# Output and down products that finish one token tile first, and a feed-forward that starts tile by tile, in a two-block transformer kernel

## Chip, cores and metric

The kernel runs on one core of a Trainium2 chip. The metric is the device time of one execution in microseconds. The engines are TensorE (PE; its weight loads are shown as PEld), VectorE (DVE), ScalarE (ACT), GpSimd (POOL) and SyncE (SP), which issues the weight transfers. Each engine runs its instructions in a fixed order.

## What is computed

256 latent tokens and 256 context tokens of width 1024 go through a first block of two layers; a second block of two other layers follows. Only the first block's products are touched by the change. Of the reference:

```python
def _post(x, f, gate, g, b):
    return _layernorm(ALPHA * x + gate * f, g, b)
def _modulate(x, shift, scale):
    return _layernorm(x) * (1.0 + scale) + shift
def _merge(o_att, o_gla, r, glu, gates, p):
    ...
    return (g_att * y_att + g_gla * y_gla + g_conv * y_conv) @ p['w_out']
def _ffn(h, p):
    return (jax.nn.silu(h @ p['w_ff_gate']) * (h @ p['w_ff_up'])) @ p['w_ff_down']
...
        if last:
            mem = _context_memory(hc, p)
        else:
            yc, mem = _context_mixer(hc, p)
            xc = _post(xc, yc, mod_c[2], ln1_g[l], ln1_b[l])
            xc = _post(xc, _ffn(_modulate(xc, mod_c[3], mod_c[4]), p), mod_c[5], ln2_g[l], ln2_b[l])
        x = _post(x, _latent_mixer(_modulate(x, sh1, sc1), mem, cos, sin, p), g1, ln1_g[l], ln1_b[l])
        x = _post(x, _ffn(_modulate(x, sh2, sc2), p), g2, ln2_g[l], ln2_b[l])
```

## The kernel before

Tokens lie on the partitions in two token tiles of 128, t0 and t1. All products are in fp32 accuracy: each operand is split into a high and a low part, and `mm3` (L216) makes three matmuls of them, hi by hi (L220), hi by lo (L221) and lo by hi (L222). A weight is loaded by SP as 512 KB (`raw`), cast to `hi` by ScalarE (L210, 128x1024) and subtracted to `lo` by VectorE (L213, two of 128x512); `weights` does that. There are four buffers for `raw`, three for `hi` and two for `lo`; with a pool and a tag given, the parts go to other memory instead.

The mixer's output product has 1024 columns in two halves c=0 and c=1, and eight blocks of 128 along the contraction, of which `weights` brings four at a time: a block (c, h) is thus half of the contraction of half of the columns. `out(c)` (L1549) is called by `post` (L1003) for c=0 and then c=1. It takes two PSUM banks, one for each token tile; in `gemm_t` each weight block is used for t0 and then t1, but the last `tail` blocks are done for t0 and then for t1. For c=1 the last two blocks are such a tail.

`post` works on each half as it is ready (`part`): L1012 multiplies by the gate, L1013 adds the residual and sums, GpSimd forms the mean (L1016), ScalarE squares (L1017), and after c=1 VectorE and GpSimd (L1023 to L1027) form the variance. `end` normalises with the wide VectorE operations L1042 and L1044. Then `ln` (L960, ScalarE's square L961, GpSimd's L274, L275, L963) and the write L969 (ScalarE, t0) or L967 (VectorE, t1) give the feed-forward's input; `to_hT` transposes it on TensorE (L984, two tiles into one PSUM bank), modulates (L989 on ScalarE, L987 on VectorE) and splits it (L310 ScalarE, L311 VectorE) into the operand `b`.

`ffn` (L1557) makes 11 features of 512 numbers, each of two weights e=0 (gate) and e=1 (up), in `g` and `t` banks, 48 matmuls of 256 columns a weight; then the down product with 22 blocks along the contraction, six weights a column half, again through `post`. In layer 0 latent and context tokens share one `ffn` (T=512), and `begin` (L1575) makes three weights' products of the context ahead. In layer 1 the context is not needed (T=256, `cn` is None), and after it the second block starts (its norm: L369, L376; transposes L385; splits L313, L314).

The pools of the mixer and of the feed-forward are opened one after the other on the same memory, so that a tile of the second waits until what lay there is read. What stands where in an engine's queue is decided when the kernel is built, by a scheduler that lays the program out over the engines and gives each engine a fixed order.

## Time and profile before

| what | value |
|---|---|
| runs of before | 2748.75, 2737.08, 2747.66 us; median 2747.66 |
| the profiled execution | 2742.06 us, span 2740.2 us |
| TensorE busy | 2640.3 us, 96% of the span |
| VectorE busy | 1955.6 us, 71% |
| ScalarE busy | 1383.8 us, 50% |
| GpSimd busy | 136.0 us, 5% |
| mean granted TensorE clock | 0.98 |

TensorE's share says little by itself, since it is near the span everywhere but at the seams between stages. Those are read in windows of some tens of microseconds, with the time in which TensorE worked and the clock that was granted to it (1.0 is 2.4 GHz, 0.5 is 1.2 GHz), and then in the timeline of an engine, where a value in brackets is the idle time ahead of an instruction and what ended it.

### The profile page before, as it was taken

What the parts mean: (1) busy time and instruction counts of PE and PEld (TensorE: products, weight loads), DVE (VectorE), ACT (ScalarE), POOL (GpSimd) and SP (SyncE); (2) the same over time, 40 slices, a digit from 0 to 9 for tenths busy, and PEclk for the clock granted to TensorE, in tenths of its full rate; (3) what the DMA queues carried; (4) which work ended last, traced back from release to release, by engine and by line L of the source; (5) the groups of instructions that cost most, each with busy time, mean ns of one, the idle gap of its engine ahead of it and who ended that gap; (6) DMA issues with size and microseconds to landing.
All of it is one profiled execution on the core that took longest, in us unless ns stands there. A gap on an engine that the chain in (4) does not pass through costs nothing.

```text
span 2740.2 us, 44882 instructions
## 1 busy us (share of the span) xinstructions
PE 2640.3 (96%) x17024; PEld 2260.7 (83%) x17024; DVE 1955.6 (71%) x3942; ACT 1383.8 (50%) x2524; POOL 136.0 (5%) x280
## 2 busy tenths in 40 slices
PE   7999999999999999999999999989999999999999
PEld 5877999977889888887797898879976699776897
DVE  4988977888866633345688997666666698556895
ACT  3555565545545422234745654544454566544663
POOL 0010011000001100002100100010010000000000
PEclk9999999999999999999999999989999999998999
DMA  7566556565535522222555433545554256542454
GB/s 255 185 229 205 170 171 217 173 205 177 178 116 193 185 85 93 93 96 91 155 170 202 156 128 116 169 154 193 186 186 156 89 185 195 173 149 80 167 192 155
DMA packets 127912, 443.29 MB, mean 162 GB/s; under 512 B 14888, under 2 KB 19112, under 8 KB 127696
## 3 DMA queue, kind: packets, MB, share of 16 engines
q1 hardware_dynamic: 127696, 440.43, 48.7%
q8 instruction: 134, 2.20, 0.3%
q14 instruction: 82, 0.67, 0.1%
HBM read 435.09 MB, written 5.28 MB: 161 GB/s over the span
## 4 chain that ended last, share of the span: by engine, by line
PE 87%; DVE 4%; DMA 3%; ACT 3%; issue 1%; POOL 1%; SPq 0%; DVEq 0%; POOLq 0%; ACTq 0%
PE g L221 20%; PE g L220 20%; PE g L222 20%; PE t L221 3%; PE t L222 3%; PE t L220 3%; DMA raw<-in_w_dram 2%; PE g L919 2%; PE t L1142 2%; PE t L1168 1%; PE t L1270 1%; PE t L1255 1%; PE t L1105 1%; DVE lo L213 1%; PE g L663 1%
## 5 line engine op out<-in xcount | busy, mean ns | idle before, releaser
L213 DVE TENSOR_TENSOR lo<-raw,hi 128x512 fp32r<-128x512 f32 (+2 forms) x1280 | 825.3, 684 | 350.4 <-issue 156.7
L210 ACT CAST hi<-raw 128x1024 fp32r<-128x1024 f32 (+2 forms) x644 | 671.9, 1045 | 723.9 <-PE g L221 252.3
L220 PE MATMUL g<-b,hi 128*128 128x256 f32 (+1 forms) x2912 | 831.1, 287 | 2.5 <-ACT hi L210 1.8
L221 PE MATMUL g<-b,hi 128*128 128x256 f32 (+1 forms) x2912 | 827.7, 286 | 2.7 <-DVE b L311 2.6
L222 PE MATMUL g<-b,lo 128*128 128x256 f32 (+1 forms) x2912 | 822.3, 287 | 1.6 <-DVE lo L213 1.6
L220 PEld LDWEIGHTS g<-b,hi 128*128 128x128 f32 x2912 | 548.2, 189 | 13.5 <-ACT b L310 2.4
L221 PEld LDWEIGHTS g<-b,hi 128*128 128x128 f32 x2912 | 548.6, 188 | 12.4 <-DVE b L311 4.3
L222 PEld LDWEIGHTS g<-b,lo 128*128 128x128 f32 x2912 | 541.5, 188 | 11.0 <-DVE lo L213 2.7
L1282 DVE SCALAR_TENSOR_TENSOR yc<-yc,vec,yc 128x256 f32<-128x256 f32 x720 | 345.7, 480 | 10.9
L221 PE MATMUL g<-lo,b 128*128 128x512 f32 (+2 forms) x712 | 271.8, 382 | 1.8 <-DVE lo L213 1.7
L220 PE MATMUL g<-hi,b 128*128 128x512 f32 (+2 forms) x712 | 253.5, 376 | 11.8 <-ACT hi L210 6.2
L222 PE MATMUL g<-hi,b 128*128 128x512 f32 (+2 forms) x712 | 264.2, 371 | 0.5 <-DVE b L314 0.4
L220 PEld LDWEIGHTS g<-hi,b 128*128 128x128 f32 x712 | 134.0, 191 | 38.6 <-ACT hi L210 7.0
L221 PEld LDWEIGHTS g<-lo,b 128*128 128x128 f32 x712 | 135.7, 191 | 30.5 <-DVE lo L213 6.3
L222 PEld LDWEIGHTS g<-hi,b 128*128 128x128 f32 x712 | 135.3, 190 | 22.2 <-DVE b L314 1.1
L220 PE MATMUL t<-b,hi 128*128 128x256 f32 (+1 forms) x336 | 111.9, 333 | 0.0
L221 PE MATMUL t<-b,hi 128*128 128x256 f32 (+1 forms) x336 | 111.9, 333 | 0.0
L222 PE MATMUL t<-b,lo 128*128 128x256 f32 (+1 forms) x336 | 111.7, 332 | 0.0
L919 PE MATMUL g<-raw,cs 128*32 128x512 f32 x384 | 84.4, 637 | 12.4 <-DMA raw<-in_w_dram 12.2
L477 DVE SCALAR_TENSOR_TENSOR s<-g,vec,s 128x255 f32<-128x255 f32 (+1 forms) x176 | 84.2, 478 | 6.0 <-ACT s L475 3.8
L221 PEld LDWEIGHTS t<-b,hi 128*128 128x128 f32 x336 | 63.2, 188 | 7.5
L220 PEld LDWEIGHTS t<-b,hi 128*128 128x128 f32 x336 | 63.1, 188 | 7.4
(421 smaller groups left out, 3924.1 us busy)
## 6 DMA issues: line engine op xcount, KB each, us to landing
raw<-in_w_dram SPq DMA_DIRECT2D x772, 512.0 KB
b<-in_row_dram SPq DMA_DIRECT2D x16, 512.0 KB
b<-in_ctx_dram SPq DMA_DIRECT2D x4, 512.0 KB
ends<-st SPq DMA_DIRECT2D x8, 256.0 KB
st<-ends SPq DMA_DIRECT2D x8, 256.0 KB
b<-in_x_dram SPq DMA_DIRECT2D x4, 512.0 KB
b<-ctx SPq DMA_DIRECT2D x4, 512.0 KB
raw<-in_w_dram SPq DMA_DIRECT2D x4, 426.0 KB
```

Of the source, the lines that this page charges most:

```text
L210: self.nc.scalar.copy(hi[:, :m], p)
L213: self.nc.vector.tensor_sub(lo[:, q], p[:, q], hi[:, q].bitcast(F32))
L220: t.matmul(ps, a[0], b[0], start=first, stop=False)
L221: t.matmul(ps, a[0], b[1], start=False, stop=False)
L222: t.matmul(ps, a[1], b[0], start=False, stop=last)
L477: nc.vector.scalar_tensor_tensor(c[:, m, j:], ps[:, m, :256 - j], cw[:, ft, 2 - j:3 - j], c[:, m, j:], op0=ALU.mult, op1=ALU.add)
L663: nc.tensor.matmul(ps[:, b], qk['nq', a * per + b][s, t * 128:t * 128 + 128], qk[kn, 0][s, :nk], start=False, stop=b == per - 1)
L919: nc.tensor.matmul(ps[32 * q:32 * q + 32], self.cs[:, h * 4 + q], raw[:, q % 2 * 512:q % 2 * 512 + 512], start=h == 0, stop=h == 1, tile_p ...
L1105: nc.tensor.matmul(p[:, h], kw[:, d, h * 128:h * 128 + 128], vg[:, h * 256:h * 256 + 256], start=True, stop=True)
L1142: nc.tensor.matmul(o, w, self.U[d][:, b * 256:b * 256 + n], start=d + i == 0, stop=d + i == 2)
L1168: nc.tensor.matmul(ps[:, a, h], G[h][b][:, a] if b < 3 else kT[:, h, ts], G[h][b][:, 2 + a], start=True, stop=True)
L1282: e.scalar_tensor_tensor(o, y[:, j:j + 256], w[:, j:j + 1], o, op0=ALU.mult, op1=ALU.add)
```

## The change

In all three full mixers `out` takes all four PSUM banks at once. The block (0, 0) is done for both token tiles; then the three other blocks (0, 1), (1, 0), (1, 1) are done for t0 and after that for t1. Their weights lie at the same time in three places: the second in pool P under 'p', the third under 'mk' and 'st', the last in the usual `hi` and `lo`. t0's products end 36 matmuls of 512 columns ahead of t1's; before, 24 in the code.

In layer 1's `ffn` a new `tile_hT` transposes and modulates one token tile at a time, and the first feature is made token tile by token tile: 96 matmuls of 256 columns as before, now with the tokens on the partitions, then four transposes back and a copy. The weights of its second half go to tiles 'z'.

In layer 1's down product the tail for c=1 is three blocks long instead of two, the last two in 'z' and 'w'; t0 ends 30 matmuls ahead instead of 18. Line numbers grow by one behind L206, by 19 behind `tile_hT`: L1012 becomes L1031, L1013 L1032, L1023 to L1025 L1042 to L1044, L1042 L1061, L1044 L1063, L1073 to L1075 L1092 to L1094.

```diff
--- before.py
+++ after.py
@@ -205,8 +205,9 @@
             for at in range(0, n, cols):
                 m = min(cols, n - at)
                 p = raw[:, at:at + m]
-                hi = self.tile(pool or self.slot(), [128, cols], F32R, tag or 'hi')
-                lo = self.tile(pool or self.W, [128, cols], F32R, tag or 'lo')
+                th, tl = tag if isinstance(tag, tuple) else (tag or 'hi', tag or 'lo')
+                hi = self.tile(pool or self.slot(), [128, cols], F32R, th)
+                lo = self.tile(pool or self.W, [128, cols], F32R, tl)
                 self.nc.scalar.copy(hi[:, :m], p)
                 for h in range(0, m, 512):
                     q = slice(h, min(m, h + 512))
@@ -261,8 +262,8 @@
         hs = list(range((n + 3) // 4))
         if n % 4:
             hs[-2:] = hs[:-3:-1]
-        own = hs[len(hs) - last:]
-        return [(4 * h, lambda h=h: self.weights(src(h), min(4, n - 4 * h), ncol, *(at if h in own else ()))) for h in hs]
+        own = dict(zip(hs[len(hs) - last:], at if at and isinstance(at[0], tuple) else (at,) * last))
+        return [(4 * h, lambda h=h: self.weights(src(h), min(4, n - 4 * h), ncol, *own.get(h, ()))) for h in hs]
 
 
     def small(self, fam, n=8):
@@ -990,6 +991,24 @@
             a = slice(kp * 2, kp * 2 + 2)
             self.split_to(hi[:, a, c0:c0 + 256], lo[:, a, c0:c0 + 256], h)
 
+    def tile_hT(self, xn, t, s, sh, sc, hi, lo):
+
+        nc = self.nc
+        ts = slice(t * 128, t * 128 + 128)
+        for c in range(2):
+            ps = self.tile(self.PT, [128, 4, 128], F32, 't')
+            h = self.tile(self.A, [128, 4, 128], F32, 'th')
+            for j in range(4):
+                k = c * 4 + j
+                nc.tensor.transpose(ps[:, j], xn[:, k * 128:k * 128 + 128], self.ident)
+                b, a = sh[:, k, s:s + 1], sc[:, k, s:s + 1]
+                if j % 2:
+                    nc.vector.tensor_scalar(h[:, j], ps[:, j], a, b, op0=ALU.mult, op1=ALU.add)
+                else:
+                    nc.scalar.activation(h[:, j], ps[:, j], AF.Identity, bias=b, scale=a)
+            a = slice(c * 4, c * 4 + 4)
+            self.split_to(hi[:, a, ts], lo[:, a, ts], h)
+
     def rows_in(self, src, tag='tm'):
         X = [self.tile(self.A, [128, D], F32, tag) for _ in range(2)]
         for t in range(2):
@@ -1546,11 +1565,26 @@
         if hook:
             hook()
 
+        pss = [[self.tile(self.PG, [128, 512], F32, 'g') for _ in range(2)] for _ in range(2)]
+
+        def product(c, h, w, t):
+            ts = slice(t * 128, t * 128 + 128)
+            for k, b in enumerate(w):
+                self.mm3(pss[c][t], [m[:, 4 * h + k, ts] for m in mh[0]], b, h + k == 0, h == 1 and k == 3)
+
         def out(c):
-            ps = [self.tile(self.PG, [128, 512], F32, 'g') for _ in range(2)]
-            tiles = self.blocks(lambda h: L.src('out', c, h), 8, 512, c, (self.P, 'p', 512))
-            self.gemm_t(ps, lambda k: (mh[0][0][:, k], mh[0][1][:, k]), tiles, tail=1 + c)
-            return ps
+
+            if c == 0:
+                w = self.weights(L.src('out', 0, 0), 4, 512)
+                for t in range(2):
+                    product(0, 0, w, t)
+                places = ((0, 1, (self.P, 'p', 512)), (1, 0, (self.P, ('mk', 'st'), 512)), (1, 1, ()))
+                ws = [(c, h, self.weights(L.src('out', c, h), 4, 512, *at)) for c, h, at in places]
+                for t in range(2):
+                    for c, h, w in ws:
+                        product(c, h, w, t)
+                return pss[0]
+            return pss[1]
         return X, self.post([(s, X)], out, self.gates[L.l, 0], L.r('ln1_g', D), L.r('ln1_b', D))[1]
 
 
@@ -1584,10 +1618,33 @@
             n = self.tile(self.P, [128, D], F32, 'tm')
             self.ln(n, X[t], t, total)
             xn.append(n)
-        self.to_hT(xn, 0, L.sh2, L.sc2, hi, lo, T - 256)
+            if cn is None:
+                self.tile_hT(n, t, 0, L.sh2, L.sc2, hi, lo)
+        if cn is not None:
+            self.to_hT(xn, 0, L.sh2, L.sc2, hi, lo, T - 256)
         del xn, n
         zs = []
-        for f in range(11):
+        if cn is None:
+
+            ws = [self.weights(L.src('up', e), 8, 256, *at) for e, at in enumerate(((), (self.P, 'z', 512)))]
+            pz = None
+            for t in range(2):
+                ts = slice(t * 128, t * 128 + 128)
+                ps = banks(0)
+                for e, w in enumerate(ws):
+                    for k in range(8):
+                        self.mm3(ps[:, e * 256:e * 256 + 256], (hi[:, k, ts], lo[:, k, ts]), w[k], e + k == 0, e == 1 and k == 7)
+                th = self.tile(self.P, [128, 512], F32, 'fth')[:, :256]
+                nc.scalar.activation(th, ps[:, :256], AF.Tanh, scale=0.5)
+                nc.vector.scalar_tensor_tensor(th, th, 1.0, ps[:, :256], op0=ALU.add, op1=ALU.mult)
+                nc.vector.tensor_mul(th, th, ps[:, 256:])
+                pz = pz or self.tile(self.PT, [128, 2, 256], F32, 't')
+                for j in range(2):
+                    nc.tensor.transpose(pz[:, j, ts], th[:, j * 128:j * 128 + 128], self.ident)
+            z = self.tile(self.P, [128, 2 * T], F32, 'z')
+            nc.scalar.copy(z, pz.rearrange("p j n -> p (j n)"))
+            zs.append(z)
+        for f in range(len(zs), 11):
             pss = []
             for e in range(2):
                 if (f, e) in ahead:
@@ -1627,8 +1684,10 @@
                     self.split_to(hi, lo, zs[k // 2], 0.5)
                     parts[k // 2] = hi, lo
                 return [a[:, k % 2 * T:(k % 2 + 1) * T] for a in parts[k // 2]]
-            tiles = self.blocks(lambda h: L.src('down', c, h), 22, 512, c, (self.P, 'z' if cn is not None else 'w'))
-            self.gemm_t(ps, Z, tiles, tail=1 + c)
+            at = (self.P, 'z') if cn is not None else ((self.P, 'z', 512), (self.P, 'w'))
+            n = 1 if cn is not None else 2
+            tiles = self.blocks(lambda h: L.src('down', c, h), 22, 512, c * n, at)
+            self.gemm_t(ps, Z, tiles, tail=1 + c * n)
             return ps
         ends = self.post(streams, down, self.gates[L.l, 1], L.r('ln2_g', D), L.r('ln2_b', D), True)
         if cn is None:
```

The scheduler's orders move with it. VectorE at the layer-1 seam, from token tile 0's last column half to its normalising; b_1720 is the residual of t0, b_1721 that of t1, `lo` and 'z' are parts of the first feature's weights. Before:

```order
L213 TENSOR_TENSOR lo_18833<-raw_18830,hi_18832 128x512 x2
L1013 SCALAR_TENSOR_TENSOR b_1721_10159,pmv_18552<-b_1721_10159,th_18639 128x512
L1012 TENSOR_TENSOR th_18736<-g_18647,b_3106_18549 128x512
L213 TENSOR_TENSOR lo_18840<-raw_18837,hi_18839 128x512 x2
L1013 SCALAR_TENSOR_TENSOR b_1720_10158,pmv_18551<-b_1720_10158,th_18736 128x512
L1023 TENSOR_SCALAR pmv_18551<-pmv_18551 128x1
L1024 TENSOR_TENSOR pmv_18551<-pmv_18551 128x1
L1025 SCALAR_TENSOR_TENSOR pmv_18551<-pmv_18551 128x1
L1012 TENSOR_TENSOR th_18765<-g_18648,b_3106_18549 128x512
L1042 SCALAR_TENSOR_TENSOR b_1720_10158<-b_1720_10158,pmv_18551,b_3145_18745 128x1024
L1013 SCALAR_TENSOR_TENSOR b_1721_10159,pmv_18552<-b_1721_10159,th_18765 128x512
L1044 SCALAR_TENSOR_TENSOR b_1720_10158,s_m_3147_18750<-b_1720_10158,pmv_18551,b_3146_18747 128x1024
```

After, the same engine from the `lo` subtraction behind t0's variance (L1042 to L1044) on; b_1724 is t0, b_1725 t1:

```order
L214 TENSOR_TENSOR lo_18859<-raw_18856,hi_18858 128x512 x2
L1061 SCALAR_TENSOR_TENSOR b_1724_10164<-b_1724_10164,pmv_18567,b_3157_18763 128x1024
L214 TENSOR_TENSOR lo_18866<-raw_18863,hi_18865 128x512 x2
L214 TENSOR_TENSOR z_18877<-raw_18870,z_18876 128x512
L214 TENSOR_TENSOR z_18883<-raw_18880,z_18882 128x512
L214 TENSOR_TENSOR z_18887<-raw_18880,z_18886 128x512
L1063 SCALAR_TENSOR_TENSOR b_1724_10164,s_m_3159_18768<-b_1724_10164,pmv_18567,b_3158_18765 128x1024
L961 TENSOR_SCALAR s_n_3162_18772<-s_m_3159_18768 128x1
L1031 TENSOR_TENSOR th_18807<-g_18564,b_3118_18565 128x512
L1006 TENSOR_SCALAR th_18784<-t_18783,mod_15249,mod_8026 128x128
L1032 SCALAR_TENSOR_TENSOR b_1725_10165,pmv_18568<-b_1725_10165,th_18807 128x512
```

The four `lo` subtractions that stood ahead of t0's L1042 of before now stand around its successor L1061, with three of the four 'z' subtractions of 128x512 behind them and ahead of L1063; and t1's L1032 stands behind an L1006, the modulation of t0's operand, which is made from t0's transposes.

TensorE at the layer-0 seam, from the end of output's products to the first product of `begin`; t_10380 to t_10410 hold the context's transposes, 16 in all, of which eight stand much earlier in the order. Before:

```order
L221 MATMUL g_10291<-gp_10323,b_1691_9889 128x512
L222 MATMUL g_10291<-gp_10322,b_1691_9889 128x512
L984 MATMUL t_10400<-cst_6_81,b_1722_10162 128x128
L984 MATMUL t_10400<-cst_6_81,b_1723_10163 128x128
L220 MATMUL g_10434<-b_1771_10378,hi_10422 128x256
L220 MATMUL g_10435<-b_1771_10378,hi_10422 128x256
L984 MATMUL t_10410<-cst_6_81,b_1722_10162 128x128
L984 MATMUL t_10410<-cst_6_81,b_1723_10163 128x128
L221 MATMUL g_10434<-b_1772_10379,hi_10422 128x256
L222 MATMUL g_10434<-b_1771_10378,lo_10423 128x256
L220 MATMUL g_10434<-b_1771_10378,hi_10422 128x256
```

After:

```order
L223 MATMUL g_10201<-hi_10293,b_1695_9895 128x512
L985 MATMUL t_10392<-cst_6_81,b_1726_10168 128x128
L985 MATMUL t_10392<-cst_6_81,b_1727_10169 128x128
L985 MATMUL t_10402<-cst_6_81,b_1726_10168 128x128
L985 MATMUL t_10402<-cst_6_81,b_1727_10169 128x128
L985 MATMUL t_10412<-cst_6_81,b_1726_10168 128x128
L985 MATMUL t_10412<-cst_6_81,b_1727_10169 128x128
L985 MATMUL t_10422<-cst_6_81,b_1726_10168 128x128
L985 MATMUL t_10422<-cst_6_81,b_1727_10169 128x128
L221 MATMUL g_10446<-b_1779_10390,hi_10434 128x256
L221 MATMUL g_10447<-b_1779_10390,hi_10434 128x256
L221 MATMUL t_10510<-b_1779_10390,z_10498 128x256
```

The eight others now all stand between output's last product and the first of `begin`; before, four of them stood inside output and four right behind it, around the first products of `begin`.

ScalarE in the gated linear attention of layer 1's context: the rows name the operations that need one of two function tables. Before:

```order
L1073 ACTIVATE ch_13561<-t_13559 128x512
L1073 ACTIVATE ch_13572<-t_13570 128x512
L1074 ACTIVATE ch_13561<-ch_13561 128x512
L1074 ACTIVATE ch_13572<-ch_13572 128x512
L1075 ACT_TABLE_LOAD
L1075 ACTIVATE ch_13561<-ch_13561 128x512
L1075 ACTIVATE ch_13572<-ch_13572 128x512
```

After:

```order
L1092 ACTIVATE ch_13573<-t_13571 128x512
L1093 ACTIVATE ch_13573<-ch_13573 128x512
L1092 ACTIVATE ch_13584<-t_13582 128x512
L1094 ACT_TABLE_LOAD
L1094 ACTIVATE ch_13573<-ch_13573 128x512
L1093 ACT_TABLE_LOAD
L1093 ACTIVATE ch_13584<-ch_13584 128x512
L1094 ACT_TABLE_LOAD
L1094 ACTIVATE ch_13584<-ch_13584 128x512
```

One table load has become three. In the latent mixer of layer 0 it is the reverse: three become one.

## Rows read from the trace of the kernel before

**Rows 1.** The page: busy time of the engines, and the chain that ended last.

```profile
PE 2640.3 (96%) x17024; PEld 2260.7 (83%) x17024; DVE 1955.6 (71%) x3942; ACT 1383.8 (50%) x2524; POOL 136.0 (5%) x280
...
PE 87%; DVE 4%; DMA 3%; ACT 3%; issue 1%; POOL 1%; SPq 0%; DVEq 0%; POOLq 0%; ACTq 0%
```

**Rows 2.** Windows: stretch, us; busy time of each engine (instructions); granted clock, DMA share, GB/s.

```profile
1805.00:1835.00 30.00, 18.10 (x83) 13.88 (x82) 18.69 (x41) 16.08 (x27) 8.47 (x18) 0.72 0.33 113
...
905.00:947.00 42.00, 37.14 (x240) 33.23 (x239) 28.88 (x59) 21.47 (x36) 8.50 (x18) 0.92 0.61 213
...
2005.00:2030.00 25.00, 18.36 (x82) 15.16 (x80) 18.83 (x56) 13.72 (x32) 5.10 (x8) 0.80 0.47 154
...
516.00:530.00 14.00, 13.19 (x63) 9.78 (x63) 9.38 (x20) 11.81 (x15) 0.00 (x0) 1.00 0.31 100
...
1360.00:1366.00 6.00, 6.00 (x26) 4.79 (x26) 4.18 (x8) 5.97 (x10) 0.00 (x0) 1.00 0.44 161
```

**Rows 3.** Timeline of TensorE, layer-1 seam: start, us, instruction, [idle before it <- releaser].

```profile
1821.63 1.39 PE L984 MATMUL t<-cst,w 128*128 128x128 f32 x4 [9.46 <-ACT w L969]
...
1825.38 3.19 PE L984 MATMUL t<-cst,w 128*128 128x128 f32 x12 [2.35 <-DVE w L967]
...
1828.56 0.58 PE L220 MATMUL g<-b,hi 128*128 128x256 f32 x1
...
1832.79 0.41 PE L220 MATMUL g<-b,hi 128*128 128x256 f32 x1
...
1833.00 0.36 PE L221 MATMUL g<-b,hi 128*128 128x256 f32 x1
...
1833.42 0.28 PE L221 MATMUL g<-b,hi 128*128 128x256 f32 x1
...
1833.54 0.28 PE L222 MATMUL g<-b,lo 128*128 128x256 f32 x1
```

**Rows 4.** Timeline of VectorE at the same seam.

```profile
1808.98 0.69 DVE L1012 TENSOR_TENSOR th<-g,b 128x512 f32<-128x512 f32 x1 [1.03 <-PE g L222]
...
1809.59 1.29 DVE L213 TENSOR_TENSOR lo<-raw,hi 128x512 fp32r<-128x512 f32 x2
...
1812.21 0.69 DVE L1012 TENSOR_TENSOR th<-g,b 128x512 f32<-128x512 f32 x1 [0.15 <-PE g L222]
...
1814.01 0.68 DVE L1013 SCALAR_TENSOR_TENSOR b<-b,th 128x512 f32<-128x512 f32 x1
...
1818.34 1.28 DVE L1044 SCALAR_TENSOR_TENSOR b<-b,pmv,b 128x1024 f32<-128x1024 f32 x1 [0.72 <-POOL pmv L1027]
```

**Rows 5.** The same timeline: GpSimd, ScalarE and VectorE in the norm.

```profile
1812.48 0.19 POOL L1026 TENSOR_TENSOR pmv<-pmv 128x1 f32<-128x1 f32 x1 [1.53 <-ACT th L1017]
...
1816.50 1.16 POOL L1026 TENSOR_TENSOR pmv<-pmv 128x1 f32<-128x1 f32 x1 [3.19 <-DVE pmv L1025]
...
1820.77 1.52 ACT L969 ACTIVATE w<-b,s_n,s_n 128x512 f32<-128x512 f32 x2 [3.33 <-POOL s_n L963]
...
1822.19 1.13 ACT L961 ACTIVATE w<-b,s_n 128x1024 f32<-128x1024 f32 x1
...
1824.78 1.00 DVE L967 TENSOR_SCALAR w<-b,s_n,s_n 128x512 f32<-128x512 f32 x2 [4.96 <-POOL s_n L963]
```

**Rows 6.** Timeline at the layer-0 seam: VectorE, TensorE.

```profile
917.21 0.99 DVE L987 TENSOR_SCALAR th<-t,mod,mod 128x256 f32<-128x256 f32 x2
...
937.14 0.44 PE L984 MATMUL t<-cst,z 128*128 128x128 f32 x2 [3.26 <-ACT z L969]
```

**Rows 7.** Timeline of ScalarE: table loads, latent mixer of layer 0 and context of layer 1.

```profile
518.90 1.28 ACT L1075 ACT_TABLE_LOAD   x1
...
1362.18 1.28 ACT L1075 ACT_TABLE_LOAD   x1
...
1363.48 1.15 ACT L1075 ACTIVATE ch<-ch 128x512 f32<-128x512 f32 x2
```

**Rows 8.** Timeline of TensorE where the second block starts.

```profile
2019.78 1.97 PE L385 MATMUL t<-cst,b 128*128 128x128 f32 x8 [5.69 <-ACT b L376]
```

## Prediction, made before the changed kernel ran

> **What bounds the kernel now.** I read the page first: TensorE is busy 96% of the span and holds 87% of the chain that ended last [rows 1]. The amount of its work does not change (four transposes of some 0.11 us more), so the time can only move where TensorE idles or runs at the lower level of its clock. Of the 2740.2 us it idles some 100. The windows then say where the change can reach [rows 2]: at the seam between the first block's layer-1 mixer and feed-forward TensorE is busy 18.10 of 30 us at a mean granted clock of 0.72; at the layer-0 seam 37.14 of 42 at 0.92; where the first block's last down product hands over to the second block 18.36 of 25 at 0.80. The waits inside them: 9.46 and 2.35 us [rows 3], 3.26 [rows 6], 5.69 [rows 8]. The reader is to see in [rows 3] that the wait is for a row tile from ScalarE or VectorE, so the chain between is the norm, and in [rows 4, 5] how long each of its links takes. The level of the clock is seen by the pitch of the 128x256 matmuls: 0.21 us until 1833, 0.115 after 1833.2 [rows 3], the levels of 1.2 and 2.4 GHz, and the low one stands behind the long wait.
>
> **Layer-1 seam.** Let O be the end of output's products, 1821.63 - 9.46 = 1812.17 [rows 3]. Before, token tile 0's last product is read at 1808.98, 3.2 us ahead of O [rows 4]. By the change it ends 36 products x 0.2325 = 8.4 us ahead in the code (the pitch of the 128x512 products, from the 3.23 us between the L1012 rows at 1808.98 and 1812.21 and the 14 products between them). That is what the change offers: 5.2 us of the 9.46. What eats it is VectorE's and ScalarE's queue, which the scheduler wrote anew. The order of before has the first feature's four lo subtractions done before O (the pair at 1809.59 is the last [rows 4]). Afterwards they wait for the lo buffers that output's last block reads to its end, and four more for the second half's weights in 'z' wait for memory of the closed mixer; VectorE's order puts all of that between token tile 0's L1023 and its L1044 (L1042 and L1063 in the new numbering). And on ScalarE the first 'z' cast stands ahead of token tile 0's second square.
>
> From the first lo subtraction that must wait: two lo 1.29, L1042's multiply 1.28, two lo 1.29, three 'z' some 1.8, L1044 1.28, the short L960: 6.9 us (the pair of 1.29 and the wide operation of 1.28 are in [rows 4]). It begins 1.4 us before O at the earliest (the first of the two lo buffers is read six products before the end) and 1.3 after it at the latest (if 'z' is free only at O: cast, subtraction, two short ones). Then from L961 to the normalising write 2.59 (1822.19 to 1824.78 [rows 5]), and from that write to the transpose 0.86 (1820.77 to 1821.63 [rows 3, 5]): 3.45. Token tile 0's transposes stand at O+9.0 to O+11.7; I take O+10.1. Before: O+9.46. The early end buys nothing.
>
> For token tile 1 it is worse. In the new order its L1013 (now L1032) stands behind an L1006, which waits for token tile 0's transposes: VectorE can do it only at about O+10.7, where before it was done at 1814.01, O+1.8 [rows 4]. From there to its transposes before took 11.37 us [rows 3, 4], 8.8 of it without the wait for ScalarE (L1044 ends at 1819.62, L961 starts at 1822.19 [rows 4, 5]); now two L1006 and two lo splits come between. So its transposes stand at O+20 to O+23 and its operand, 3.2 us later as before (1825.38 to 1828.56 [rows 3]), at O+23 to O+26. TensorE has only token tile 0's 48 products of the first feature meanwhile. They start at O+13.3 and take 5.6 to 10.2 us by the two pitches. Then 48 more: from O+25, at the mean of the pitches 7.9 us, the first feature ends at O+33. Before: 96 x 0.114 from 1828.56 = O+16.4, plus 2 us for the 20 products at the low level, is O+29.4. The difference is +3.6; its bounds are -1 (operand at O+23, high level) and +6.8 (O+26, low level).
>
> The 0.19 and 1.16 us of the same one-column GpSimd operation L1026 [rows 5] matter here: the long one ran beside L1042, a VectorE operation with two wide inputs in SBUF, the short one ahead of one. The change puts eight subtractions of that kind into the norm, so GpSimd's few steps may take 1 us longer each; that is inside the bounds above. The Trainium skill, SBUF — State Buffer, section "Who interferes with whom", says that such a VectorE instruction and a GpSimd instruction that reads SBUF block each other for the whole instruction; the trace agrees (1.16 against 0.19), and by that rule alone the term would go to its upper end.
>
> **Layer-0 seam.** Here TensorE loses 3.26 us and two waits of 0.6, 4.4 in all, and 3.4 more by the low clock (42 us at 0.92 are 6.7 us at half) [rows 2, 6]. After the change the eight context transposes that stood in and right behind output's end all stand behind its last product, and four VectorE modulations (0.50 each by the pair of 0.99 [rows 6]), a 'z' and two lo subtractions (0.60 each) stand ahead of the first split that the products wait for: 3.8 us, of which transposes and the first four products hide about 1.4. That is a new wait of some 2.4 to 3.4 us, with the low clock possibly behind it. In return the products of `begin` end as much later and cover token tiles 0 and 1: 2.4 to 3.4 us of the 4.4 go. I take 0; ends -4 (the clock's loss goes too) and +4 (it comes twice).
>
> **Table loads.** ScalarE's activations of the gated linear attention come out in another order. In the latent mixer of layer 0 two of three loads vanish, in layer 1's context one becomes three. One load is 1.28 us, and the next activation starts 0.02 us behind it [rows 7]. The first gain is bounded by TensorE's idle time there, 0.81 of 14 us [rows 2]: -0.6. The second costs ScalarE 2.6 us where it is busy 5.97 of 6.00 us and TensorE has no idle [rows 2], so most of it comes through: +2.0 (0 to 2.6). Together +1.4. The Trainium skill, ScalarE: Activation LUTs, section "What ACT_TABLE_LOAD costs", gives some 1.28 us for the load and 1.38 more to drain; by it the term would be about twice as large, but the trace shows no drain.
>
> **Down to the second block.** Token tile 0's products end 30 instead of 18 products ahead, 2.8 us. If all its links move with it, the wait of 5.69 [rows 8] becomes 2.9. But token tile 1's links do not move, and in the new order the second block's small element operations and one table load share ScalarE and VectorE with token tile 0. Ends: -2.8 and +1.3 (one load). I take 0, for the wait behind it is then token tile 1's.
>
> **Sum.** 3.6 + 0 + 1.4 + 0 = +5.0 us. The profiled execution took 2742.06; the three runs have a median of 2747.66 and reach from 2737.08 to 2748.75. The mean of these four is 2743.9; I put the sum on that: 2749 us.
>
> **The rivals.**
> *The offered gain comes.* Token tile 0's chain isn't held: 5.2 us at the layer-1 seam, 2.35 behind 48 products, 2 of the clock, 2.8 at the second block: -12.4, about 2731. For it: each of these waits is real. Against it: the order of VectorE, in which eight subtractions stand in the chain, is fixed at build. Chance 0.15.
> *Slower, by the clock.* The seam is now cut into three waits instead of one. If TensorE stays at the low level over all 96 products of the first feature, 76 x 0.10 = 7.5 us come in place of the 2.5 already counted; if the new wait at layer 0 brings the low clock without removing the old, 3.4; with token tile 1's operand at O+26, 1 more: 2749 + 5.0 + 3.4 + 1 and the table loads' upper end 0.6, about 2759, with run scatter to 2764. It decides when over half of the 96 run at a pitch of 0.21. For it: in [rows 3] the low level lasts 4.6 us beyond the end of the waits. Chance 0.2.
> *Nothing changes.* What the waits lose in one place the cover gives back in another: 2744. That is also the case in which ScalarE's and VectorE's queues on the chip run ahead far enough that the order is harmless. Chance 0.2.
> *The forecast*, 2745 to 2754: 0.45.
>
> **How the numbers follow.** A difference of 0.5%, 13.7 us, is about what a measurement of this kernel can tell from no change. Faster by that needs the first rival whole: half of its 0.15, 0.07. Slower by that needs the second at its upper half and some of the forecast's tail: 0.15. The rest, 0.78, is within. The range reaches from 2737, which leaves out most of the first rival, to 2762, which leaves out the upper end of the second.
>
> **What would show it.** Right: token tile 0's first transposes about 10 us behind output's last product, with subtractions on VectorE in between; a second wait for token tile 1 after 48 products of the first feature, with VectorE idle ahead of its L1032; a wait of 2 to 3 us at the start of the layer-0 `begin`, and the 3.26 us wait mostly gone; three loads at the layer-1 context. Wrong: transposes within 6 us of output's end, or the two halves of the first feature without a wait between them.

## The result, and the profile after

The changed kernel takes 2763.61 us (median of 10 runs, 2752.49 to 2774.21) beside 2746.48 of the kernel before on the same chip (10 runs, 2737.08 to 2750.53): a ratio of 1.0067, 95% interval 1.0049 to 1.0084. It is slower by some 17 us, where 2749 us with a range of 2737 to 2762 had been predicted. The profiled execution took 2770.79 us, its span 2769.0.

The page of the changed kernel, busy time, answers to [rows 1]:

```profile
PE 2657.3 (96%) x17028; PEld 2276.3 (82%) x17028; DVE 1956.3 (71%) x3948; ACT 1386.1 (50%) x2539; POOL 136.5 (5%) x280
```

It tells little, as before: TensorE is 17 us longer "busy" with four more instructions, so part of the loss lies inside the products (a low clock, a wider pitch) and only part in waits. Windows of the changed kernel (stretch, busy time of PE, PEld, DVE, ACT, POOL, granted clock, DMA share, GB/s): the layer-1 seam from the end of output's products, the context of layer 1, the layer-0 seam, the hand-over to the second block.

```profile
1825.10:1859.00 33.90, 17.03 (x85) 13.94 (x86) 17.76 (x37) 14.09 (x26) 5.47 (x10) 0.65 0.24 78
1301.80:1392.00 90.20, 77.81 (x390) 61.60 (x390) 55.73 (x108) 62.74 (x105) 13.70 (x37) 0.91 0.46 146
905.00:947.00 42.00, 37.38 (x227) 32.75 (x225) 27.62 (x56) 21.17 (x34) 8.91 (x18) 0.92 0.63 222
2037.40:2062.00 24.60, 18.28 (x86) 15.24 (x87) 18.31 (x59) 17.55 (x38) 3.72 (x6) 0.79 0.51 173
```

The first two of them in the kernel before, between the same events:

```profile
1812.20:1846.00 33.80, 21.93 (x147) 19.40 (x148) 20.02 (x37) 15.22 (x25) 5.70 (x10) 0.75 0.30 94
1297.40:1380.96 83.56, 74.57 (x390) 59.57 (x390) 55.76 (x107) 60.17 (x103) 12.93 (x37) 0.94 0.51 159
```

In the 34 us behind output's end TensorE gets through 85 instructions instead of 147, at a mean clock of 0.65 instead of 0.75. For the same 390 instructions the context of layer 1 takes 90.20 us instead of 83.56. The two other places hardly moved. The loss lies between the end of layer 0 and the last down product: that stretch took 716.7 us in the profile of before and 735.6 in that of the changed kernel, and 720.3 and 735.4 when both were profiled once more. So it is 15 to 19 us longer, and the medians differ by 17.

Timeline of TensorE at the layer-1 seam of the changed kernel (start, us, instruction, idle before it and what ended it), against [rows 3]; L1003 are the transposes of the new `tile_hT`. Output ended at 1836.98 - 11.96 = 1825.02, which is O below.

```profile
1836.98 0.47 PE L1003 MATMUL t<-cst,w 128*128 128x128 f32 x1 [11.96 <-ACT w L970]
...
1843.08 0.58 PE L221 MATMUL g<-hi,b 128*128 128x256 f32 x1 [1.52 <-ACT b L311]
...
1844.66 0.58 PE L223 MATMUL g<-hi,b 128*128 128x256 f32 x1 [0.78 <-DVE b L312]
...
1847.61 0.41 PE L221 MATMUL g<-hi,b 128*128 128x256 f32 x1
...
1848.36 0.28 PE L222 MATMUL g<-lo,b 128*128 128x256 f32 x1
...
1850.71 0.27 PE L1003 MATMUL t<-cst,w 128*128 128x128 f32 x1
...
1855.14 0.58 PE L221 MATMUL g<-hi,b 128*128 128x256 f32 x1 [0.72 <-ACT b L311]
```

The reader is to see four things: a first wait of 11.96 us instead of 9.46; 6.1 us from t0's first transpose to its first product; the products at a pitch of 0.21 us until 1848, then 0.12; and only 0.72 us of waiting ahead of t1's first product, because t0's 48 products had started so late. A fifth shows in the granted clock: with t1's transposes TensorE had waited again (0.40, 0.23 and 0.72 us), and then the clock fell to the low level a second time. Windows of TensorE alone, behind that wait and over all 96 products of the first feature:

```profile
1855.00:1858.40 3.40, 3.26 (x15) 0.51 0.00 0
1843.09:1862.54 19.45, 17.32 (x108) 0.78 0.09 29
```

The timeline of ScalarE, with one issue of SyncE, and of VectorE there, against [rows 4, 5]:

```profile
1824.27 1.65 ACT L211 CAST z<-raw 128x512 fp32r<-128x512 f32 x3
1828.74 1.04 ACT L211 CAST hi<-raw 128x1024 fp32r<-128x1024 f32 x1 [2.82 <-DMA raw<-in_w_dram]
1832.55 1.04 ACT L211 CAST hi<-raw 128x1024 fp32r<-128x1024 f32 x1 [2.77 <-DMA raw<-in_w_dram]
1833.50 1.14 ACT L962 ACTIVATE w<-b,s_n 128x1024 f32<-128x1024 f32 x1
...
1827.54 0.33 SPq L190 DMA_DIRECT2D raw<-in_w_dram  x1
...
1823.79 1.29 DVE L214 TENSOR_TENSOR lo<-raw,hi 128x512 fp32r<-128x512 f32 x2
1825.00 1.27 DVE L1061 SCALAR_TENSOR_TENSOR b<-b,pmv,b 128x1024 f32<-128x1024 f32 x1
1826.19 1.28 DVE L214 TENSOR_TENSOR lo<-raw,hi 128x512 fp32r<-128x512 f32 x2
1827.40 1.88 DVE L214 TENSOR_TENSOR z<-raw,z 128x512 fp32r<-128x512 f32 x3
1829.20 1.27 DVE L1063 SCALAR_TENSOR_TENSOR b<-b,pmv,b 128x1024 f32<-128x1024 f32 x1
...
1838.55 0.41 DVE L1006 TENSOR_SCALAR th<-t,mod,mod 128x128 f32<-128x128 f32 x1 [7.28 <-PE t L1003]
1838.87 0.68 DVE L1032 SCALAR_TENSOR_TENSOR b<-b,th 128x512 f32<-128x512 f32 x1
...
1847.91 1.00 DVE L968 TENSOR_SCALAR w<-b,s_n,s_n 128x512 f32<-128x512 f32 x2 [2.64 <-POOL s_n L964]
```

VectorE does what the order said: t0's row is done at 1829.20 + 1.27 = 1830.5. But ScalarE starts its square L962 only at 1833.50. Two casts of a later feature's weights stand ahead of it, and each has waited 2.8 us for its load. The load of the second is issued at 1827.54, 0.07 us behind the end of the second pair of `lo` subtractions (1826.19 + 1.28 = 1827.47), the last readers of an earlier `raw` buffer, and lands 4.9 us later.

### The profile page after: what moved, and what is told of

Read it like the earlier page. It is cut to its first block, busy times and chain, and to the rows that moved or that the text cites. A ratio compares the mean times of both kernels' runs of the same rounds, so it can differ in the third digit from the quotient of the medians.

```text
span 2769.0 us, 44892 instructions
## 1 busy us (share of the span) xinstructions
PE 2657.3 (96%) x17028; PEld 2276.3 (82%) x17028; DVE 1956.3 (71%) x3948; ACT 1386.1 (50%) x2539; POOL 136.5 (5%) x280
## 4 chain that ended last, share of the span: by engine, by line
PE 86%; DVE 4%; DMA 4%; ACT 3%; issue 2%; POOL 1%; SPq 0%; DVEq 0%; POOLq 0%; ACTq 0%
PE g L222 20%; PE g L221 20%; PE g L223 20%; DMA raw<-in_w_dram 3%; PE t L221 3%; PE t L223 3%; PE t L222 3%; PE g L920 2%; PE t L1161 2%; PE t L1187 1%; PE t L1289 1%; PE t L1124 1%; PE t L1274 1%; DVE lo L214 1%; PE t L1196 1%
## 5 line engine op out<-in xcount | busy, mean ns | idle before, releaser
L214 DVE TENSOR_TENSOR lo<-raw,hi 128x512 fp32r<-128x512 f32 x1262 | 813.4, 683 | 360.8 <-issue 161.6
L211 ACT CAST hi<-raw 128x1024 fp32r<-128x1024 f32 x635 | 662.4, 1045 | 722.7 <-PE g L222 286.1
L223 PE MATMUL t<-b,lo 128*128 128x512 f32 (+1 forms) x320 | 108.1, 338 | 0.0
L221 PE MATMUL t<-b,hi 128*128 128x512 f32 (+1 forms) x320 | 108.1, 338 | 0.0
L222 PE MATMUL t<-b,hi 128*128 128x512 f32 (+1 forms) x320 | 108.1, 338 | 0.0
L223 PEld LDWEIGHTS t<-b,lo 128*128 128x128 f32 x320 | 60.3, 189 | 7.2
L222 PEld LDWEIGHTS t<-b,hi 128*128 128x128 f32 x320 | 60.4, 189 | 7.2
```

The costliest lines, as they stand in the source:

```text
L211: self.nc.scalar.copy(hi[:, :m], p)
L214: self.nc.vector.tensor_sub(lo[:, q], p[:, q], hi[:, q].bitcast(F32))
L221: t.matmul(ps, a[0], b[0], start=first, stop=False)
L222: t.matmul(ps, a[0], b[1], start=False, stop=False)
L223: t.matmul(ps, a[1], b[0], start=False, stop=last)
```

## The experiments

"Seam" is the time from O to the tanh of the second feature (all of the first feature's 96 products and 48 more are then done); "context" is the stretch of layer 1 shown above. All from one profile each; the ratio is to the kernel before, timed in the same batch. A seam from one profile is good to 1 or 2 us: b_again, down_only and before_gates have the output product and the first feature of before and show 37.4, 35.6 and 35.8. What differs is how far the low clock reached into the first feature: 18 of its 96 products came at a pitch of 0.21 us or wider (slow, below) in before, 22 in b_again, 5 in down_only and in before_gates.

| kernel | ratio (95%) | context | first wait | seam | O to the last down product |
|---|---|---|---|---|---|
| before | | 83.6 | 9.46 | 36.8 | 201.9 |
| b_again | 1.0007 (0.9991 to 1.0024) | 85.4 | 9.46 | 37.4 | 203.1 |
| after | 1.0067 (1.0049 to 1.0084) | 90.2 | 11.96 | 44.2 | 212.3 |
| a_again | 1.0067 (1.0048 to 1.0086) | 90.6 | 11.74 | 45.0 | 212.8 |
| out_only | 1.0029 (1.0011 to 1.0047) | 90.5 | 10.58 | 36.4 | 201.9 |
| ffn_only | 1.0048 (1.0024 to 1.0071) | 86.6 | 9.56 | 42.0 | 210.3 |
| down_only | 1.0013 (0.9997 to 1.0030) | 83.6 | 9.46 | 35.6 | 200.5 |
| old_feature | 1.0087 (1.0053 to 1.0120) | 89.6 | 7.08 | 43.1 | 211.9 |
| old_operand | 1.0074 (1.0049 to 1.0100) | 91.0 | 13.95 | 39.7 | 208.0 |
| before_gates | 1.0111 (1.0094 to 1.0128) | 80.5 | 9.45 | 35.8 | 204.8 |
| after_gates | 1.0165 (1.0126 to 1.0204) | 82.6 | 11.68 | 44.2 | 216.3 |
| all_scalar | 1.0091 (1.0061 to 1.0121) | 89.3 | 12.53 | 46.7 | 214.8 |
| swap | 1.0078 (1.0052 to 1.0103) | 91.5 | 10.11 | 41.1 | 209.2 |
| scalar_swap | 1.0077 (1.0049 to 1.0106) | 87.0 | 9.77 | 41.1 | 209.2 |
| raw_own | 1.0076 (1.0052 to 1.0099) | 89.5 | 7.08 | 38.2 | 206.1 |
| raw_own_swap | 1.0048 (1.0026 to 1.0069) | 89.2 | 7.98 | 39.1 | 207.2 |
| old_feature_swap | 1.0073 (1.0044 to 1.0103) | 88.8 | 7.99 | 45.5 | 214.4 |

**The two kernels once more** (a_again, b_again), without an edit, for what of a profile repeats.

> The changed kernel unchanged, to see what of its profile comes again. Its first profile lost 28.7 us against the one of before; by sight 10 to 11 us of that at the layer-1 seam, 6 at the layer-1 context, some 13 because products of 256 columns in the layer-1 feed-forward and in the second block came every 0.118 us where before had 0.113. Theory A (the pitch belongs to the program): 0.118 again in the second block's feed-forward, 1.004 to 1.009 of before. Theory B (the pitch belongs to the execution): a profile that may have 0.113 there, and single times spread over 10 us and more. Either way the layer-1 seam shows a wait of 11 to 12 us again.

> The kernel of before unchanged, as the measure of scatter: ratio 1.000 within 0.003. Theory A: 0.113 us pitch in the second block's feed-forward again. Theory B: in this profile it may be 0.118.

The seam and the context come back within 2 us in each kernel, and the ratio is the same. What does not come back lies elsewhere: from the end of the last down product to TensorE's last instruction 725.0 and 711.0 us in the two profiles of the changed kernel, 719.5 and 714.8 in those of before. So stages are compared, not single spans.

**One part of the change alone**: the kernel before with the new `out` (out_only), with the new start of `ffn` (ffn_only), with the longer tail of `down` (down_only).

```diff
 out_only:   - tiles = self.blocks(lambda h: L.src('out', c, h), 8, 512, c, (self.P, 'p', 512))
             + places = ((0, 1, (self.P, 'p', 512)), (1, 0, (self.P, ('mk', 'st'), 512)), (1, 1, ()))
...
 ffn_only:   + self.tile_hT(n, t, 0, L.sh2, L.sc2, hi, lo)
...
 down_only:  + at = (self.P, 'z') if cn is not None else ((self.P, 'z', 512), (self.P, 'w'))
```

> Only the output products are changed (all four banks at once, token tile 0 first, weights in three places). The theory of the prediction, queues: with the feed-forward as before there are no subtractions of a second half's weights in 'z' in the norm, but the lo buffers are still held by output's last block; layer-1 seam +0 to +4, layer-0 seam 0, layer-1 context +2 to +6 if its order has three table loads: 1.001 to 1.004. Rival, the offered gain comes when output is alone: seam -4 to -5, 0.997 to 0.999.

> Only the layer-1 feed-forward's start is changed (operand and first feature token tile by token tile, second half's weights in 'z'). Queues: token tile 0 ends 3 us ahead only, the 'z' conversions still stand in the norm, the order in layers 0 and the context is as before: +3 to +6 at the layer-1 seam, 1.001 to 1.003. Rival, the cover pays: the second wait of 2.35 us falls away and the seam is 2 to 5 us shorter, 0.998 to 0.999.

> The kernel of before with the longer tail of the layer-1 down product alone. The wait at the second block falls from 5.69 to 4.75 us as in the changed kernel: -1 us, ratio 0.999 to 1.000 (0.998 to 1.002 measured). The pitch of the layer-1 feed-forward's products stays 0.115 us if it hangs on the seam's order, and may be 0.118 if any change of the program can set it: then +3 and 1.001.

The parts add up: 0.29%, 0.48% and 0.13% to 0.90 where the whole has 0.67, which their intervals allow. The new `out` shows no cost at the seam (36.4), but there the clock helped: its first wait is 1.1 us longer, its first product starts at O+17.5 instead of O+16.4, and only 4 of the 96 products are slow. It costs 5 to 7 us in the context of layer 1, a place that its lines do not touch; the new start of `ffn` costs 5 us at the seam. Both together cost 7.5. down_only has the one gain: the wait of 5.69 [rows 8] is 4.75 there, and so it is in every kernel with that part:

```profile
2042.11 1.97 PE L386 MATMUL t<-cst,b 128*128 128x128 f32 x8 [4.74 <-ACT b L377]
```

**One part of the new start undone**: the first feature as before (old_feature), the operand from `to_hT` for both tiles (old_operand).

```diff
 old_feature
-        if cn is None:
+        if False:
             ws = [self.weights(L.src('up', e), 8, 256, *at) for e, at in enumerate(((), (self.P, 'z', 512)))]
...
 old_operand
-            if cn is None:
-                self.tile_hT(n, t, 0, L.sh2, L.sc2, hi, lo)
-        if cn is not None:
-            self.to_hT(xn, 0, L.sh2, L.sc2, hi, lo, T - 256)
+        self.to_hT(xn, 0, L.sh2, L.sc2, hi, lo, T - 256)
```

> The changed kernel with the first feature of the layer-1 feed-forward made as before (weight by weight over both token tiles, no 'z'), the operand still made token tile by token tile. In the changed kernel the stretch from output's end to the second feature's tanh takes 44.2 to 45.0 us, before 36.8. Theory queue ('z' conversions in token tile 0's norm): the first wait falls from 11.7 to about 9 us, but token tile 1's L1032 still stands behind token tile 0's operand, and both halves of the feature wait for both tiles: 39 to 42 us. Theory feature (the new form of the first feature itself, with its transposes, is what costs): back to 37. The products of the other features come at 0.115 us if the new form sets the slow pitch, at 0.118 if not. Ratio to before 1.003 to 1.006.

> The changed kernel with the operand of the layer-1 feed-forward made as before (both token tiles transposed into one bank, modulated and split together); the first feature still goes token tile by token tile with 'z'. Theory queue: the first wait stays near 11 us or grows by token tile 1's L1032 in between (0.6), but token tile 1 is no longer held; output's end to the second feature's tanh 40 to 43 us. Theory operand (L1032 behind L1006 is most of it): 37 to 39. Ratio 1.003 to 1.006.

Old_feature's 43.1 is outside both expectations, old_operand's 39.7 between its two. With the operand made for both tiles the seam falls by 5 us although the first wait rises to 13.95, so the length of the first wait alone does not tell the cost. Most of the 5 us is the clock, as TensorE's window over the first feature's 96 products shows:

```profile
1847.22:1859.23 12.01, 12.01 (x100) 0.98 0.17 52
```

There is no wait between these products, and 3 of them are slow instead of 32 (40 in a_again). At 0.095 us each (0.213 - 0.118) that is 2.8 to 3.5 us; the waits for t1's operand make up the rest.

Timeline of old_feature, ScalarE, VectorE and TensorE:

```profile
1828.56 1.15 ACT L962 ACTIVATE w<-b,s_n 128x1024 f32<-128x1024 f32 x1 [2.40 <-DVE s_n L961]
...
1833.61 0.41 DVE L1006 TENSOR_SCALAR th<-t,mod,mod 128x128 f32<-128x128 f32 x1 [4.48 <-PE t L1003]
...
1832.04 0.48 PE L1003 MATMUL t<-cst,w 128*128 128x128 f32 x1 [7.08 <-ACT w L970]
...
1843.58 3.96 PE L1003 MATMUL t<-cst,w 128*128 128x128 f32 x8 [6.96 <-DVE w L968]
```

Here no cast waits ahead of the square, and t0's wait is 7.08. But VectorE idles 4.48 us ahead of L1006 with t1's L1032 behind it, and t1's wait of 6.96 is in the open, since no product of t0 covers it.

**The table loads.** In both kernels the logarithms of both token tiles are tied behind both exponentials by a one-column operand, so that all gates need one load of each table (23 loads in the program instead of 35).

```diff
+        one = self.small('gt', 1)
+        nc.vector.tensor_scalar(one, a[1][:, :1], 0.0, 1.0, op0=ALU.mult, op1=ALU.add)
...
-        nc.scalar.activation(a, a, AF.Ln, bias=1.0)
+            nc.scalar.activation(a[t], a[t], AF.Ln, bias=one)
```

> The changed kernel, with both token tiles' logarithms of the gates in the gated linear attention tied behind both exponentials (a one-column operand), so that each pair of token tiles needs one table load for the logarithm and not three: 23 loads instead of 35. Theory loads: the layer-1 context, 64.1 to 64.9 us from its first pair to its third product wait where before has 57.7 to 59.6, falls by 4 to 6, and the layer-1 first pair by 2; ratio 1.002 to 1.005. If something else moved there, 64 again and 1.006.

> The kernel of before with the same tie, 23 loads instead of 35. If table loads come through where ScalarE is full: 0.997 to 0.999. If TensorE has cover nearly everywhere: 1.000, within 0.002.

With equal loads the context's difference falls from 5 to 7 us to 2.1 (82.6 against 80.5), so that the loads make most of it. The other kernels say the same: where the context has six loads (before, b_again, ffn_only, down_only) it takes 83.6 to 86.6 us, where it has eight 87.0 to 91.5. Against what was expected, both kernels with the tie are slow: by 2772 and 2786 us they lose over 20. In other mixers the first tile's gates now come late, as on TensorE in before_gates (the second line is from its page):

```profile
166.65 0.39 PE L1149 MATMUL t<-U,lgh 128*128 128x256 f32 x1 [2.34 <-ACT gp L1157]
...
PE 2669.2 (96%) x17024; PEld 2290.9 (83%) x17024; DVE 1959.9 (71%) x3950; ACT 1370.7 (50%) x2512; POOL 133.9 (5%) x280
```

But that wait is not the loss. TensorE idles 99.9 us in before_gates and 99.9 in before (2769.1 - 2669.2 and 2740.2 - 2640.3), at the same mean clock of 0.98; the 29 us lie inside the products, for the same 17024 instructions. Why they come at a wider pitch there stays open (see the last section).

What the extra loads do in the changed kernel's context (ScalarE, VectorE, TensorE; the window behind it):

```profile
1371.26 1.28 ACT L1093 ACT_TABLE_LOAD   x1
...
1373.21 1.28 ACT L1094 ACT_TABLE_LOAD   x1
...
1379.51 1.28 ACT L1107 ACT_TABLE_LOAD   x1
1380.80 0.60 ACT L1107 ACTIVATE ch<-t 128x512 f32<-128x512 f32 x1
...
1381.43 1.29 DVE L1108 TENSOR_TENSOR ch<-ch,k 128x512 f32<-128x512 f32 x2 [0.50 <-ACT ch L1107]
...
1382.18 1.22 PE L1124 MATMUL t<-k,ch 128*128 128x256 f32 x2 [2.34 <-DVE ch L1108]
...
1376.00:1392.00 16.00, 12.88 (x60) 9.67 (x58) 9.87 (x19) 10.08 (x20) 0.00 (x0) 0.79 0.37 121
```

The same place in the kernel before (TensorE; window):

```profile
1373.74 3.70 PE L1105 MATMUL t<-k,ch 128*128 128x256 f32 x16
...
1365.00:1381.00 16.00, 15.59 (x86) 12.51 (x84) 12.23 (x23) 11.85 (x21) 0.00 (x0) 1.00 0.60 185
```

TensorE stands for 2.34 us where the kernel before has no wait. The granted clock over the 16 us from 1376 is 0.79, where before has 1.00; that is 6.7 us at the low level, of which half, 3.4, is lost. 2.3 and 3.4 are 5.7, between the 5.2 and the 6.6 of the context's difference in the two pairs of profiles.

**VectorE's share.** All of `tile_hT`'s modulations on ScalarE, so that no L1006 is in VectorE's queue (all_scalar); output's last two weight blocks exchanged in their places, so that other memory comes free first (swap); both (scalar_swap).

```diff
 all_scalar
-                if j % 2:
-                    nc.vector.tensor_scalar(h[:, j], ps[:, j], a, b, op0=ALU.mult, op1=ALU.add)
-                else:
-                    nc.scalar.activation(h[:, j], ps[:, j], AF.Identity, bias=b, scale=a)
+                nc.scalar.activation(h[:, j], ps[:, j], AF.Identity, bias=b, scale=a)
...
 swap
-                places = ((0, 1, (self.P, 'p', 512)), (1, 0, (self.P, ('mk', 'st'), 512)), (1, 1, ()))
+                places = ((0, 1, (self.P, 'p', 512)), (1, 0, ()), (1, 1, (self.P, ('mk', 'st'), 512)))
```

> The changed kernel with all modulations of the layer-1 operand on ScalarE, so that VectorE's order has no L1006 ahead of token tile 1's L1032; its eight subtractions stay in token tile 0's norm. So far, output's end to the second feature's tanh: before 36.8 to 37.4, changed 44.2 to 45.0 us. Theory 'token tile 1 held behind token tile 0's operand is the larger part': 40 to 42, first wait near 11.7 as in the changed kernel. Theory 'the subtractions in token tile 0's norm are the larger part': 43.5 to 45, ScalarE's four more modulations eating what VectorE gains. Ratio 1.004 to 1.006 by the first, 1.007 by the second.

> The changed kernel with two of output's weight places exchanged: the third block in the usual hi and lo, the last in 'mk' and 'st', so that the lo buffers come free 12 products earlier and the first feature's four lo subtractions stand ahead of the variance of token tile 0; three of the four 'z' subtractions stay in its norm or move behind L1063, and L1032 stays behind L1006. Theory subtractions: first wait 7 to 8 us instead of 11.7, second feature's tanh at 40 to 42 us. Theory token tile 1 held: the first wait shrinks, but token tile 1's moves with it by the same 4 us, also 40 to 42; the two part in the next kernel. If neither holds, 44 to 45. A stall of TensorE of 1 to 2 us may come inside output, where the third block's lo now waits for the first's.

> Both of the two repairs. If the two holds add (each 3 to 4 us), the second feature's tanh comes at 36 to 39 us, as in the kernel before, and the ratio is 1.002 to 1.004, what is left being the layer-1 context (some 5 us) and the slower pitch of the products in the layer-1 feed-forward (0.118 instead of 0.115 us, some 3 us). If only one of them was the bound: 40 to 42 and 1.004 to 1.006.

Without an L1006 on VectorE the seam is no shorter (46.7, outside both expectations, and 41.1 beside 41.1 with the exchange). That does not clear t1's place behind L1006, to which the prediction gave most of the loss, since all_scalar only moves the hold. Its timeline (O is 1825.23; L1029 is the L1032 of after, L1033 its L1036, L1058 its L1061):

```profile
1831.52 0.69 DVE L1029 SCALAR_TENSOR_TENSOR b<-b,th 128x512 f32<-128x512 f32 x1
1841.55 1.29 DVE L1058 SCALAR_TENSOR_TENSOR b<-b,pmv,b 128x1024 f32<-128x1024 f32 x1 [8.76 <-ACT th L1033]
...
1840.71 0.71 ACT L1033 ACTIVATE th<-b,pmv 128x512 f32<-128x512 f32 x1
```

t1's sum is done 7.6 us earlier (O+6.3 instead of O+13.9), but its square then stands in ScalarE's queue behind t0's modulations, and VectorE idles 8.76 us for it. What speaks against the hold is the trace of the changed kernel: t1's row is written (L968, at 1847.91) by O+23.9, 1.8 us before TensorE, busy with t0's products, comes to t1's transposes at O+25.7. The exchange takes 3 to 4 us off: 1.6 to 1.9 of the first wait and, with 19 slow products instead of 32 to 40, 1.2 to 2.0 of the clock. One of the two casts then waits 1.78 us instead of 2.77.

**The casts that wait for loads.** The second half's weights are loaded into tiles of their own pool instead of the four `raw` buffers (raw_own), the same with the exchange (raw_own_swap), and the exchange with the old first feature (old_feature_swap).

```diff
-        raw = self.tile(self.W, [128, 1024], F32, 'raw')
+        raw = self.tile(*getattr(self, 'rawat', (self.W,)), [128, 1024], F32, 'w' if hasattr(self, 'rawat') else 'raw')
...
+            self.rawat = (self.P,)
+            ws.append(self.weights(L.src('up', 1), 8, 256, self.P, 'z', 512))
```

> The changed kernel with one edit: the weights of the first feature's second half are loaded into tiles of their own pool instead of the four raw buffers, so that ScalarE's two casts of them no longer wait for a load that itself waits for a buffer. Theory 1 (ScalarE's in-order queue: casts that wait for loads stand ahead of token tile 0's square, 2.8 us in the profile of the changed kernel): the first wait of TensorE behind output falls from 11.7 - 12.0 to 8.5 - 9.5 us, the tanh of the second feature stands at 41 - 42.5 us behind output's end instead of 44 - 45, the whole 2 - 3 us less. Theory 2 (VectorE's subtractions hold the chain, as the prediction had it): the squares come no earlier, the wait stays at 11 - 12 and the tanh at 44 - 45. Theory 3 (what bounds is token tile 1 and the low clock behind the wait): the first wait falls, but the tanh stays at 44 - 45.

> The same loads in tiles of their own pool, and besides the places of output's last two weight blocks exchanged (the one edit that brought the seam down so far: first wait 10.11, tanh of the second feature 41.1 us behind output's end, one cast still waiting 1.78 us for its load). Theory 1 (casts waiting for loads): the wait falls by the 1.78 left, to 8 - 9 us, the tanh stands at 39 - 40. Theory 2 (VectorE's subtractions): no change against the exchange alone, 10 and 41. Theory 3 (token tile 1 and the clock): the first wait falls, the tanh stays at 41. The kernel would still be slower than before by the 5 - 6 us of layer 1's context, which this edit does not touch: a ratio of 1.003 - 1.006.

> The changed kernel with the first feature as before and output's last two weight blocks exchanged: nothing waits for a load ahead of a square, and no 'z' subtractions stand in the norm, but token tile 1's VectorE step L1032 still stands behind an L1006 that waits for token tile 0's transposes. Theory 1 (casts waiting for loads): the best of the variants, first wait 6 - 7, and a second one of at most 5. Theory 3 (token tile 1 behind L1006): first wait 6 - 7, second wait 6 - 8 again as with the old first feature alone (7.08 and 6.96), tanh of the second feature at 42 - 43. Theory 2: with the early lo subtractions ahead of output's end the wait of token tile 0 goes below 6.5.

Timeline of raw_own, VectorE, ScalarE, TensorE (its O is 1822.47):

```profile
1823.35 1.29 DVE L214 TENSOR_TENSOR lo<-raw,hi 128x512 fp32r<-128x512 f32 x2
1824.56 1.28 DVE L1063 SCALAR_TENSOR_TENSOR b<-b,pmv,b 128x1024 f32<-128x1024 f32 x1
...
1826.07 1.15 ACT L962 ACTIVATE w<-b,s_n 128x1024 f32<-128x1024 f32 x1 [2.40 <-DVE s_n L961]
...
1829.55 0.47 PE L1003 MATMUL t<-cst,w 128*128 128x128 f32 x1 [7.08 <-ACT w L970]
...
1835.65 0.58 PE L221 MATMUL g<-hi,b 128*128 128x256 f32 x1 [1.52 <-ACT b L311]
```

The square starts 0.2 us behind L1063's end instead of 3.0, and the 'z' subtractions are gone from between `lo` and L1063, which ends at O+3.4 instead of O+5.5. Together that is the 4.9 us by which the first wait falls: 2.8 ScalarE's casts, 2.0 VectorE's subtractions. The edit moved both, so theories 1 and 2 each hold a part of it, and the seam is 6 us shorter; the rest of the 6 is the clock, 19 slow products instead of 32 and 40. Theory 3 falls as far as this kernel goes; in old_feature_swap the second wait of 6.96 is there again, and 45.5. With the exchange the wait and the seam (7.98 and 39.1) are what theory 1 gave, but they are no better than in raw_own alone.

The median of raw_own doesn't show the 6 us: 1.0076 with an interval that reaches down to 1.0052, where 1.0045 would have been expected. That of raw_own_swap, whose seam is nearly as short, does: 1.0048 (1.0026 to 1.0069). So the repair is shown in the profiles and not settled in the times; the profile of raw_own has 721.6 us behind the last down product, in code that the edits leave alone and that took 711.0 to 725.6 us in all profiles but the two with the tie. No variant of the changed kernel beats the kernel before, and none is expected to: the best seam, 38.2, is still behind 36.8 and 37.4.

## Why the prediction was wrong

The direction was right and the sum too small: +5.0 us by the steps, some +15 in the profiles (context 5.2 to 6.6, seam 7.5, features behind it 1.6 to 3.1, second block -1) and 17 in the medians. The steps that failed are ScalarE's casts and the slower operand at the layer-1 seam, and the low clock behind the new wait in the context.

**Layer-1 seam, +3.6 predicted, +7.4 to 7.6 measured.** The mechanism was the right one, t0's early end is eaten by what the order puts into its norm. Of its steps:
- *The subtractions*: the first `lo` at O-1.2 (predicted O-1.4 to O+1.3), L1063's end at O+5.5. Right, at the early end.
- *The offer*: 3.23 us over 14 products is a pitch of 0.2307 us, not 0.2325, and 36 of them 8.3 us; it changes nothing.
- *"From L961 to the normalising write 2.59"*, right behind VectorE's row: failed. From the square to the transposes it took 3.48 us, as predicted (3.45), but the square started 3.0 us behind the row. The cast that the prediction named stands ahead of an earlier square of t0 (L1036); the two ahead of L962 it did not look for, and ScalarE's queue had no price. ScalarE waited there 2.8 us for a load, and the load for a `raw` buffer that the late subtractions held. t0's transposes stood at O+12.0 instead of O+10.1, outside its bounds.
- *"Its operand, 3.2 us later as before"*, with t0's products from O+13.3: failed. `tile_hT` takes 6.1 us from first transpose to first product in after and in raw_own alike, with waits for modulation and split of 0.46, 0.45 and 1.52 us between, and 0.78 more behind the first product. Products started at O+18.1.
- *t1's hold behind L1006*: there, but late products of t0 covered it. Its transposes came at O+25.7 (predicted O+20 to 23), its wait was 0.72. No run takes the hold away and leaves the rest as it is. The first feature's last product starts at O+37.5 (38.2 in a_again), predicted O+33; before O+29.8 (30.1), predicted 29.4.
- *The clock*: 32 of the 96 products ran at a pitch of 0.21 us or wider (40 in a_again), against 18 and 22 in the two profiles of before. The rival "by the clock" wanted over half; it came to 1 to 2 us of its 7.5 (10 to 22 more slow products at 0.095 us).

**Layer-0 seam, 0 predicted**: from the end of TensorE's products ahead of L985 in the mixer before it (851.95 us in before) to the end of layer 0 it is 445.54 and 445.37 us against 445.41 and 445.32. Timeline of TensorE, changed kernel, against [rows 6]:

```profile
921.52 0.44 PE L985 MATMUL t<-cst,b 128*128 128x128 f32 x2 [0.79 <-ACT th L990]
922.82 0.51 PE L221 MATMUL g<-b,hi 128*128 128x256 f32 x2 [0.87 <-ACT b L311]
925.93 0.58 PE L222 MATMUL g<-b,hi 128*128 128x256 f32 x1 [2.12 <-DVE b L312]
945.82 0.89 PE L985 MATMUL t<-cst,z 128*128 128x128 f32 x4 [0.44 <-ACT th L990]
```

3.8 us of waits at the start of `begin`, and the wait of 3.26 is 0.44: as predicted, one for the other.

**Table loads, +1.4 predicted.** In the latent mixer the -0.6 can't be told from scatter: the stretch took 199.36 us before and 199.47 after, 201.33 and 197.55 in b_again and a_again. In the context +2.0 was predicted and 5.2 to 6.6 measured. The wait itself, 2.34, is inside the bound of 2.6; the failed step is that the term ended there. A wait was priced without the low clock behind it, 3.4 us, although the prediction had done just that at the seam. The Trainium skill, ScalarE: Activation LUTs, section "What ACT_TABLE_LOAD costs", with its 1.38 us to drain for each load, would have given a larger term, but for the wrong reason: the activation at 1380.80 starts 0.01 us behind the end of the load at 1379.51 + 1.28, so the trace shows no drain.

**Hand-over to the second block, 0 predicted**: 5.69 became 4.74, a gain of 1 us, inside the bounds.

**Not in the prediction**: the features behind the first, below.

## What to carry to other kernels

When work is moved ahead in one engine's order, follow what the other engines have in front of the next link: a cast that waits for a load in a fixed queue delays a norm step that has nothing to do with it, and the load may wait for a buffer that the moved work holds. A wait on TensorE has a second price, the products that run at the low clock behind it (here 3.4 us behind 2.3), and it belongs into each term that makes a new wait. It also moves a stage by 1 to 3 us from one profile to the next, so count the slow products before a difference is put down to an order. And a change of one stage's allocation can reorder another stage: compare the order over the whole program, not only at the seam.
